# A row-wise gradient of an 8192 x 8192 matrix: partitions that hold 64 consecutive rows instead of six

## The chip, the core and the metric

The kernel runs on one core of a Trainium2 chip. Times are microseconds of device time. The kernel before takes 1245.38 us, the median of three runs (1245.34 to 1245.58). All other numbers come from one profiled execution of the same kernel.

The core has on-chip memory of 128 partitions. Its compute engines work on all partitions at once; here VectorE (DVE in the profile) and GpSimd (POOL) are used. Data come from and go to the chip's main memory by DMA: 16 DMA engines move the data of a transfer together, and SyncE (SP) issues the transfers one after the other on one queue.

## The reference

```python
def setup_inputs():
    return {"x": np.random.randn(8192, 8192).astype(np.float32)}

def reference(x):
    return np.gradient(x, axis=1)
```

Each row is treated by itself. In the inside of a row, out[j] = (x[j+1] - x[j-1]) / 2; at its two ends, out[0] = x[1] - x[0] and out[8191] = x[8191] - x[8190]. Input and output are 256 MB (268.44 million bytes) each, and a row is 32 KB.

## The kernel before

A tile holds two rows (R = 2) in each of 128 partitions: 256 rows, 64 KB a partition, 8.39 MB in all. There are nsets = 32 tiles. The function `sets` (lines 26 to 32) says which rows of the matrix a tile holds: three tiles (NB = 3) form a group, and a group takes 768 consecutive rows, of which each partition has six, rows 6p to 6p+5 of the group. The first tile of the group takes the first two of the six, the second the next two, the third the last two. So within a tile the partitions' pieces lie 6 x 32 KB = 192 KB apart in main memory, and each piece is one run of 64 KB. The last group has only two tiles, hence four rows a partition and 128 KB between pieces. Input and output use the same layout.

On the chip there are three buffers, slot0 to slot2, used in turn. For each tile:

- `load` (line 53) issues one transfer for the tile on SP (line 55). It waits until the store from the same buffer, three tiles earlier, has landed.
- GpSimd computes the four end values of each partition (two rows, two ends) into a small tile `ends` (line 65). It waits for the load.
- VectorE does the whole inside with one custom instruction (line 71): the difference of the buffer shifted by two elements, times 0.5. It writes the same buffer 64 elements further to the front, and waits for GpSimd.
- The four end values are put in their places over the result (line 82), by GpSimd for 12 of the tiles and by VectorE for the other 20.
- SP issues the store (line 84) as soon as they are there.

The order of the work is written out by hand. SP issues three loads, then three stores, each when its tile is done, then the next three loads, and so on: after every third tile the next three loads follow (lines 86 to 88). All 64 transfers go through SP's one queue in this order. The helper `chain` (line 43) only tells the tile framework which earlier steps an instruction must wait for.

Of the kernel before, what the change touches and what calls it, by code (L numbers as in the profile page):

```python
# [1 line left out]

# [4 lines left out]


@with_exitstack
def kernel(  # L10
    ctx: ExitStack,
    tc: tile.TileContext,
    x: bass.AP,
    out: bass.AP,
):
    nc = tc.nc
    P = nc.NUM_PARTITIONS
    n, m = x.shape
    R = 2
    NB = 3  # L20
    SH = 64
    W = R * m
    nsets = n // (P * R)
    f32 = x.dtype

    def sets(a):
        found = []
        for first in range(0, nsets, NB):
            q = min(NB, nsets - first)
            rows = a[first * P * R : (first + q) * P * R, :].rearrange("(p q) m -> p (q m)", p=P)  # L30
            found += [rows[:, k * W : (k + 1) * W] for k in range(q)]
        return found

    x_sets, out_sets = sets(x), sets(out)

    pool = ctx.enter_context(tc.tile_pool(name="pool", bufs=1))
    pad = pool.tile([P, 32], f32, name="pad", tag="pad")
    slots = [pool.tile([P, SH + W], f32, name=f"slot{k}", tag=f"slot{k}") for k in range(NB)]
    ends = pool.tile([P, nsets, R, 2], f32, name="ends", tag="ends")
    loads, stores = [], [None] * nsets  # L40
    in_front = {}

    def chain(i, ins, *needed):
        group, engine = f"slot{i % NB}", ins.ins.engine
        keep = [o.ins for o in needed]
        if in_front.get(engine, (None,))[0] == group:
            keep.append(in_front[engine][1])
        tc.declare_no_dep(ins.ins, group=group, keep=keep, reason="implied by the needed step")
        tc.add_to_no_dep_group(group, ins.ins)
        in_front[engine] = group, ins.ins  # L50
        return ins

    def load(i):
        b = slots[i % NB]
        ins = nc.sync.dma_start(out=b[:, SH : SH + W], in_=x_sets[i])  # L55
        loads.append(chain(i, ins, *([stores[i - NB]] if i >= NB else [])))

    with tc.manual_schedule():
        for i in range(NB):
            load(i)  # L60
        for i in range(nsets):
            b = slots[i % NB]
            xin = b[:, SH : SH + W].rearrange("p (t m) -> p t m", m=m)

            ins = nc.gpsimd.tensor_sub(  # L65
                out=ends[:, i, :, :],
                in0=xin[:, :, 1 : m : m - 2],
                in1=xin[:, :, 0 : m - 1 : m - 2],
            )
            at = [chain(i, ins, loads[i])]  # L70
            ins = nc.vector._custom_dve(  # L71
                dve_ops.TENSOR_TENSOR_REDUCE_SUB_MAX,
                out=b[:, 1 : W - 1],
                in0=b[:, SH + 2 : SH + W],
                in1=b[:, SH : SH + W - 2],
                s0=0.0,
                s1=0.5,
            )
            halved = chain(i, ins, *at)
            res = b[:, 0:W].rearrange("p (t m) -> p t m", m=m)  # L80
            placer = nc.gpsimd if i % 5 in (1, 3) and i < nsets - 2 else nc.vector
            ins = placer.tensor_copy(out=res[:, :, 0 : m : m - 1], in_=ends[:, i, :, :])  # L82
            placed = chain(i, ins, halved)
            ins = nc.sync.dma_start(out=out_sets[i], in_=b[:, 0:W])
            stores[i] = chain(i, ins, placed)
            if i % NB == NB - 1:
                for k in range(i + 1, min(i + 1 + NB, nsets)):
                    load(k)


# [1 line left out]
_INS = ['x']  # L92
_OUTS = [((8192, 8192), 'float32')]


# [23 lines left out]
```

## Time and profile before

| what | value |
|---|---|
| median of three runs | 1245.38 us |
| the profiled execution, its own time | 1246.23 us |
| its span in the profile | 1244.3 us |
| VectorE busy | 554.6 us, 45% of the span |
| GpSimd busy | 8.9 us, 1% |
| data moved | 268.44 MB read, 268.44 MB written |
| mean rate | 431 GB/s |
| issue to landing, median | load 57.9 us, store 40.4 us |

The span is what the profiler saw from the first to the last instruction; 1.93 us of the execution's own time lie around it. The profile's second part cuts the span in 40 slices and gives for each the busy share of an engine in tenths, so that 9 means 90% or more; for DMA it is the mean over the 16 engines. The third part adds up the packets, the pieces into which the transfers were cut. The DMA view can be asked for a window of time and then gives the same lines for the packets that start in it, also cut in 40 slices. Waits are listed as who waited for whom: total time, number of times, longest.

### The profile page before, as it was taken

The page shows a single profiled execution, that of the slowest core. Times are in us where ns is not written, and L with a number is a line of the kernel's source. Part 1 is how long each engine was busy: PE and PEld are TensorE (multiplying, and loading weights), DVE is VectorE, ACT ScalarE, POOL GpSimd, SP SyncE. Part 2 cuts the span into 40 slices and gives each one's busy share as a digit, 9 for nine tenths or more (in the row PEclk, how much of TensorE's full clock was granted, in tenths as well). Part 3 has the DMA queues.
Part 4 walks back from the last instruction along what each step waited for, and adds up shares of the span by engine and source line. Part 5 has one row for each costly group of instructions (what it writes and reads, how often), then busy time and mean ns, then how long its engine had stood idle before and what let it go on. Part 6 is the DMA issues. An engine that isn't in the chain of part 4 may idle for free.

```text
span 1244.3 us, 237 instructions
## 1 busy us (share of the span) xinstructions
DVE 554.6 (45%) x52; POOL 8.9 (1%) x48
## 2 busy tenths in 40 slices
DVE  2850583069009603850582079009603840591082
POOL 0000000000000000000000000000000000000000
DMA  9999999999999999999999999999999999999999
GB/s 404 438 436 423 421 438 438 438 438 436 434 423 430 434 438 438 430 436 432 428 434 436 432 436 434 438 436 430 432 428 438 436 434 438 434 434 430 430 409 404
DMA packets 9217, 536.88 MB, mean 431 GB/s; under 512 B 1024, under 2 KB 1024, under 8 KB 1024
## 3 DMA queue, kind: packets, MB, share of 16 engines
q1 hardware_dynamic: 9216, 536.88, 99.8%
q14 instruction: 1, 0.01, 0.0%
HBM read 268.44 MB, written 268.44 MB: 431 GB/s over the span
## 4 chain that ended last, share of the span: by engine, by line
another core or an unknown queue 74%; DVE 18%; DMA 3%; issue 2%; POOL 1%; SPq 0%; POOLq 0%
DVE slot L71 18%; DMA slot<-in_x_dram 3%; POOL ends L65 0%; POOL slot L82 0%; SPq L55 0%; POOLq L114 0%; DVE slot L82 0%
## 5 line engine op out<-in xcount | busy, mean ns | idle before, releaser
L71 DVE CUSTOM_DVE_ANT_0 slot<-slot 128x16382 f32<-128x16382 f32 x32 | 551.2, 17224 | 667.2 <-POOL ends L65 667.2
L65 POOL TENSOR_TENSOR ends<-slot 128x4 f32<-128x4 f32 x32 | 6.4, 200 | 988.1 <-DMA slot<-in_x_dram 988.1
L82 POOL COPY slot<-ends 128x4 f32<-128x4 f32 x12 | 2.3, 192 | 207.9 <-DVE slot L71 207.9
L82 DVE COPY slot<-ends 128x4 f32<-128x4 f32 x20 | 3.4, 172 | 0.7
L103 POOL MEMSET const-bfloat16-1.0<- 128x1 bf16 x1 | 0.1, 102 | 0.0
L103 POOL MEMSET const-uint8-127<- 128x1 uint8 x1 | 0.1, 102 | 0.0
L103 POOL MEMSET const-float32-0.0<- 128x1 f32 x1 | 0.1, 99 | 0.2 <-issue 0.2
L103 POOL MEMSET const-float32-1.0<- 128x1 f32 x1 | 0.1, 99 | 0.0
## 6 DMA issues: line engine op xcount, KB each, us to landing
slot<-in_x_dram SPq DMA_DIRECT2D x32, 57.9
out_dram<-slot SPq DMA_DIRECT2D x32, 40.4
```

The lines of the kernel that those rows point to most:

```text
L65: ins = nc.gpsimd.tensor_sub(out=ends[:, i, :, :], in0=xin[:, :, 1 : m : m - 2], in1=xin[:, :, 0 : m - 1 : m - 2],)
L71: ins = nc.vector._custom_dve(dve_ops.TENSOR_TENSOR_REDUCE_SUB_MAX, out=b[:, 1 : W - 1], in0=b[:, SH + 2 : SH + W], in1=b[:, SH : SH + W - 2],
L82: ins = placer.tensor_copy(out=res[:, :, 0 : m : m - 1], in_=ends[:, i, :, :])
L103: nc = _bacc.Bacc("TRN2", target_bir_lowering=False, num_devices=1)
```

## The change

The function `sets` loses its loop over groups. The whole matrix is laid out at once: partition p holds rows 64p to 64p+63, and tile k takes rows 2k and 2k+1 of those 64 in every partition. A tile's piece in a partition is still one run of 64 KB, but the pieces of neighbouring partitions are now 64 x 32 KB = 2 MB apart, in the input and in the output, for all 32 tiles. Nothing else is changed; the instructions on each engine and their order are the same, and the lines of the kernel after `sets` move up by four.

```diff
     def sets(a):
-        found = []
-        for first in range(0, nsets, NB):
-            q = min(NB, nsets - first)
-            rows = a[first * P * R : (first + q) * P * R, :].rearrange("(p q) m -> p (q m)", p=P)
-            found += [rows[:, k * W : (k + 1) * W] for k in range(q)]
-        return found
+        rows = a.rearrange("(p q) m -> p (q m)", p=P)
+        return [rows[:, k * W : (k + 1) * W] for k in range(nsets)]
 
     x_sets, out_sets = sets(x), sets(out)
```

## The prediction

> **What bounds the kernel now.** I read the page first, then the DMA view in short windows, then the waits.
>
> The page, parts 1 to 3 and 5:
>
> ```profile
> span 1244.3 us, 237 instructions
> DVE 554.6 (45%) x52; POOL 8.9 (1%) x48
> DMA  9999999999999999999999999999999999999999
> ...
> DMA packets 9217, 536.88 MB, mean 431 GB/s; under 512 B 1024, under 2 KB 1024, under 8 KB 1024
> q1 hardware_dynamic: 9216, 536.88, 99.8%
> ...
> L71 DVE CUSTOM_DVE_ANT_0 slot<-slot 128x16382 f32<-128x16382 f32 x32 | 551.2, 17224 | 667.2 <-POOL ends L65 667.2
> ```
>
> The 16 DMA engines are busy for 99.8% of the span in every slice; VectorE, the only compute engine with real work, is busy for 45%. Of the 9216 packets 1024 are tiny (under 512 B, 16 for each of 64 transfers). The other 8192 carry the 536.87 MB: 65,536 bytes each, one packet for one partition's two rows. Each of the 16 engines so moves 512 of them.
>
> The DMA view in four windows: the first wave of loads, the loads behind it, a stretch in the middle, and the last store.
>
> ```profile
> DMA packets 16, 1.05 MB, mean 350 GB/s; under 512 B 0, under 2 KB 0, under 8 KB 0
> q1 hardware_dynamic: 16, 1.05, 104.6%
> ...
> DMA packets 112, 7.34 MB, mean 465 GB/s; under 512 B 0, under 2 KB 0, under 8 KB 0
> q1 hardware_dynamic: 112, 7.34, 107.2%
> ...
> DMA  0999000999000999000999000999000999000999
> DMA packets 128, 7.34 MB, mean 459 GB/s; under 512 B 16, under 2 KB 16, under 8 KB 16
> ...
> DMA packets 160, 8.39 MB, mean 387 GB/s; under 512 B 32, under 2 KB 32, under 8 KB 32
> q1 hardware_dynamic: 160, 8.39, 89.2%
> ```
>
> Packets are counted where they start, so share x window x 16 engines / packets is the mean duration of one.
> - 1.2 to 4.2 us (first wave, one packet per engine): 1.046 x 3.0 x 16 / 16 = 3.138 us.
> - 4.2 to 20 us: 1.072 x 15.8 x 16 / 112 = 2.420 us.
> - 300 to 316 us: the digits repeat every six slices of 0.4 us, three busy and three empty. All 16 engines start their packets within about half a packet's time of each other, every 2.4 us: they walk in step.
> - 1222.6 to 1244.3 us (the last store, 128 large packets): 0.892 x 21.7 x 16 / 128 = 2.420 us.
>
> 512 x 2.420 = 1239.0 us of the 1244.3 us span. So the bound is each engine's own 2.42 us for 64 KB, and the memory behind it never shows except in two waves: the first loads, and the first stores, at 57.9 to 59.2 us:
>
> ```profile
> DMA packets 16, 1.05 MB, mean 807 GB/s; under 512 B 0, under 2 KB 0, under 8 KB 0
> q1 hardware_dynamic: 16, 1.05, 264.4%
> ```
>
> 2.644 x 1.3 x 16 / 16 = 3.437 us per packet.
>
> The waits of SP's queue show what hangs on landings:
>
> ```profile
> SPq L84 <- DVE slot L82: 525.5, 20, 55.9
> SPq L55 <- DMA out_dram<-slot: 372.9, 29, 19.1
> ```
>
> SP waits often, but always with transfers already queued behind which it waits, since the DMA row has no gap.
>
> **The change part by part.**
>
> *What stays.* The 32 loads, 32 stores and all compute instructions stand in the same order on every engine; each transfer is still 128 runs of 64 KB, so still 512 large packets per engine. No wait, buffer or instruction is added or taken: 0 us. That VectorE needs 17.22 us per tile is hidden under the 2 x 8 x 2.42 = 38.7 us that its load and store take; longer packets only widen this cover. SP's waits on landings stretch in proportion to the packets, with the queue no emptier.
>
> *The last two tiles* had runs 128 KB apart and now have them 2 MB apart; the other 30 go from 192 KB to 2 MB. These are one edit: the addresses that the 16 engines touch at the same moment.
>
> *Price of the new addresses.* The 128 partitions of a transfer now begin at multiples of 2 MB: whatever share of them an engine has, 16 engines in step read addresses equal in their low 21 bits. Before, with 192 KB = 3 x 64 KB, those bits differed from engine to engine. If memory spreads addresses over its parts by such bits, the engines now meet in the same few parts. No row of before shows a 2 MB step, so I bound it.
> - From below: the last store, with a power of two (128 KB) between runs, has 2.420 us per packet, as the tiles with 192 KB. By this row the change costs 0, and no gain is possible beyond the 1244.3 - 1239.0 = 5.3 us that are not plain packet time; of those at least the 1.2 us before the first transfer starts remain, so 4.1 us at most.
> - From above: the only packets that memory rather than the engine lengthened are the two waves: 3.138 - 2.420 = 0.718 us more for loads, 3.437 - 2.420 = 1.017 us more for stores. At the store wave's price throughout it is 512 x 1.017 = 520.7 us.
>
> I take the loads' price for all packets. The waves are the rows where 16 engines press on memory that cannot serve them at once, the condition that the change would make permanent; the 128 KB row has a step 16 times smaller. A part of each wave is a cost of beginning or of turning round that steady traffic would not repeat, so I take the lower of the two, also for stores. The first wave has already paid: 511 x 0.718 = 366.9 us.
>
> *Weighed against the Trainium skill.* The Trainium skill, "DMA: Bandwidth & Descriptors", section "Latency and other measured facts", gives for copies of 128-partition tiles 207 GB/s per direction at a row pitch of 512 KiB, 164 at 2 MiB, 103 at 4 MiB and 214 where the pitch is padded; it calls channel aliasing its inference. By the ratio 214/164 the time would be an estimated 1245.4 x 1.305 = 1625 us. Its runs were 16 KiB, not 64 KB, and no run of before has such a pitch; the 128 KB row neither bears it out nor speaks against it.
>
> *Sum.* The profiled execution took 1246.23 us, 1.93 us of it outside its span of 1244.3 us. 1246.2 + 366.9 = 1613.1 us; the median of the runs shown, 1245.38 us, lies 0.85 us lower, so I forecast 1612 us. The last large packet still ends the program: its wave is in the 512.
>
> **The rivals.**
>
> *Only a part of the traffic pays.* (a) Stores may be taken up by buffers and loads alone pay: 255 x 0.718 = 183 us, 1428 us. (b) The step may break: an engine that is held back falls behind the others, reaches a given address later, and meets nobody. For it: at 600 to 616 us the pulses of before have widened over the whole period (next fence), by drift alone. If only the first three loads and three stores pay (48 packets per engine): 47 x 0.718 = 34 us, 1279 us; of these the loads alone: 23 x 0.718 = 17 us, 1262 us. Against it: at 300 us the engines were still in step within about 1.2 us of 2.42, after 120 packets each, and a crowd of engines that waits for one place moves on together.
>
> ```profile
> DMA  9997709997709997709993909993739993739993
> ```
>
> *The pitch does not matter* (not slower). The memory has headroom that the engines' 431 GB/s do not use up, or mixes high address bits so that 2 MB steps spread as 192 KB steps do. For it: the 128 KB row, and 2.42 us all through the loads behind the first wave, though the engines are in step. Then each packet stays 2.42 us and the time stays 1245.4 us. It decides as soon as memory serves 16 such streams at 16 x 65,536 B / 2.42 us = 433 GB/s; below that every shortfall lands on the end, for nothing covers DMA time. A gain could only come from shorter waves: two waves of before cost 0.7 and 1.0 us, and without all of it and the other gaps 1246.2 - 4.1 - 0.85 = 1241.3 us is the floor.
>
> *Dearer than the waves.* If more than 16 requests pile up at one place, a packet may exceed 3.437 us: over 1245.4 + 520.7 = 1766 us. Nothing in the trace holds such a packet on average, so this has little weight.
>
> *The change does not do what it says.* Then the 64 KB runs would be cut up; but a tile's two rows are adjacent in the new layout too, so I give this nothing.
>
> **How the numbers follow.** This kernel's runs agree within 0.02%; about 0.2% (2.5 us) is what a measurement can tell from no change. All traffic pays about a wave's price (1430 to 1766 us; likeliest, 1612): 0.56. A part pays (1262 to 1430): 0.24. A trace of it, 1248 to 1262: 0.02. The pitch does not matter: 0.09. Faster, down to 1241: 0.03. Dearer than 1766: 0.06. The range 1262 to 1766 holds 0.80 and ends on the two bounds worked out above. Slower is 0.56 + 0.24 + 0.02 + 0.06 = 0.88, same 0.09, faster 0.03.
>
> **What would show it.** Right: packets still 9216 and 536.88 MB, DMA digits still 9 throughout, but GB/s per slice near 536.88 MB / 1610 us = 333 instead of 434, packets of about 3.1 us by the same working, VectorE's busy time unchanged at 554.6 us with its share down to about 34%, and SP's wait on landed stores up by some 30%. Case (a) would show loads at 3.1 us and stores at 2.42 in the windows; case (b) a low GB/s in the first slices that climbs back to 434. Wrong: packets at 2.42 us in every window; or stretches in which the DMA row falls below 9, which would mean that a wait and not the packets holds the end.

## The result: 4.7% slower, a sixth of the loss that was forecast

The changed kernel takes 1304.97 us (median of six runs, 1294.97 to 1311.88) against 1245.74 us for the kernel before (six runs, 1245.34 to 1246.48). The ratio is 1.0466, with a 95% interval from 1.0425 to 1.0508. The forecast was 1612 us. The direction was right and the time lies in the range, but the loss is 59 us and not 367. The runs of the changed kernel also scatter over 17 us, those of the kernel before over 1 us.

The page of the changed kernel, parts 1 to 3 and the costliest group:

```profile
span 1298.8 us, 237 instructions
DVE 554.6 (43%) x52; POOL 8.8 (1%) x48
DMA  9999999999999999999999999999999999999988
GB/s 355 412 416 383 400 434 434 386 432 430 434 400 430 422 426 406 428 432 404 432 428 436 402 428 434 414 418 436 424 418 436 422 432 410 434 434 416 420 299 303
DMA packets 9217, 536.88 MB, mean 413 GB/s; under 512 B 1024, under 2 KB 1024, under 8 KB 1024
q1 hardware_dynamic: 9216, 536.88, 99.2%
...
L67 DVE CUSTOM_DVE_ANT_0 slot<-slot 128x16382 f32<-128x16382 f32 x32 | 551.2, 17224 | 711.1 <-POOL ends L61 711.1
```

Packets, bytes and VectorE's time are what they were, and the DMA engines are still busy 99.2% of a longer span (1298.8 us, 54.5 us more). So the packets became longer, as forecast; but only some of them. The row of GB/s shows which: it is low in the first slices (355), climbs to the old 434, dips in every third or fourth slice (383, 386, 400, 406, 404 are the first), and ends with 299 and 303.

The DMA view of the changed kernel in four windows: the first wave (1.2 to 4.2 us), the packets behind it (4.2 to 20), a stretch in the middle (190 to 206) and one in the last two stores (1252 to 1268). Packets are counted where they start.

```profile
DMA packets 16, 1.05 MB, mean 350 GB/s; under 512 B 0, under 2 KB 0, under 8 KB 0
q1 hardware_dynamic: 16, 1.05, 115.9%
...
DMA packets 92, 6.03 MB, mean 382 GB/s; under 512 B 0, under 2 KB 0, under 8 KB 0
q1 hardware_dynamic: 92, 6.03, 101.6%
...
DMA  9709399909399909399909399909379909379939
DMA packets 116, 6.95 MB, mean 434 GB/s; under 512 B 10, under 2 KB 10, under 8 KB 10
q1 hardware_dynamic: 116, 6.95, 100.2%
...
DMA  0049940000999000009994000999900009999400
DMA packets 80, 5.24 MB, mean 328 GB/s; under 512 B 0, under 2 KB 0, under 8 KB 0
q1 hardware_dynamic: 80, 5.24, 97.7%
```

Share x window x 16 / large packets gives 3.477 us in the first wave (3.138 before), 1.016 x 15.8 x 16 / 92 = 2.792 us behind it, 1.002 x 16 x 16 / 106 = 2.420 us in the middle, and 0.977 x 16 x 16 / 80 = 3.126 us in the last stores. The two DMA rows show the difference between the last two. In the middle the 16 engines start at all times of the 2.4 us period: only single slices are empty. In the last stores there are three to five slices of 0.4 us in which nobody starts: the engines are in step. The same 2 MB step costs nothing in the one state and 0.7 us a packet in the other.

The time of each packet beyond 2.418 us, added up from the single packet records of the trace, gives 49.5 us per engine (2.9 us before). Of these 13.9 us fall in the first 140 us: 6.7 us in the first three loads, 5.3 us where the first three stores give way to loads, the rest in these stores. Another 9.9 us fall in the last two stores, and 25.7 us in between, all of it where the direction changes: 21.4 us at the nine places where stores give way to loads, 4.3 us where loads give way to stores. So about 31 of the 49.5 us lie at changes of direction. There the packets are longer than in step; around the first such change, from 122 to 132 us:

```profile
DMA packets 52, 2.62 MB, mean 262 GB/s; under 512 B 12, under 2 KB 12, under 8 KB 12
q1 hardware_dynamic: 52, 2.62, 101.7%
```

1.017 x 10 x 16 / 40 = 4.07 us, and the longest single packet there takes 5.2 us. The loss falls from change to change, from 5.3 us at the first and 3.5 at the second to 1.5 us at the last from stores to loads, while the landings of one transfer on the 16 engines spread from 4 to 16 us.

Ahead of the last two stores the engines are idle for 7.3 us on average (1.7 us before), as the store of the last tile but one waits for VectorE while the engines, now apart, run out of loads. 46.6 + 5.6 = 52.2 us of the 54.5 us are found so. Of the rest, the records show 0.7 us more of idle time at the end and 0.6 us more in the first 10 us; about 1 us stays unplaced.

SP's waits grew as the packets did:

```profile
SPq L80 <- DVE slot L78: 537.7, 20, 58.3
SPq L51 <- DMA out_dram<-slot: 395.8, 29, 23.2
```

The second was 372.9 us: 6% more, not the 30% that the forecast named.

### The profile page after: what moved, and what is told of

It reads as the page before. It is cut to its first block, busy times and chain, and to the rows that moved or that the text cites. A ratio compares the mean times of both kernels' runs of the same rounds, so it can differ in the third digit from the quotient of the medians.

```text
span 1298.8 us, 237 instructions
## 1 busy us (share of the span) xinstructions
DVE 554.6 (43%) x52; POOL 8.8 (1%) x48
## 2 busy tenths in 40 slices
DMA packets 9217, 536.88 MB, mean 413 GB/s; under 512 B 1024, under 2 KB 1024, under 8 KB 1024
## 3 DMA queue, kind: packets, MB, share of 16 engines
q1 hardware_dynamic: 9216, 536.88, 99.2%
## 4 chain that ended last, share of the span: by engine, by line
another core or an unknown queue 74%; DVE 17%; DMA 4%; issue 2%; POOL 1%; SPq 0%; POOLq 0%
DVE slot L67 17%; DMA slot<-in_x_dram 4%; POOL ends L61 0%; POOL slot L78 0%; SPq L51 0%; POOLq L110 0%; DVE slot L78 0%
```

## The experiments

Three theories are tested. Theory A: the step of 2 MB lengthens a packet only while the 16 engines start together; they drift apart by themselves, and meet again after every dry queue, that is, whenever all transfers that were issued are done. Theory B: what costs is the reach of a transfer over the whole 256 MB, whatever the step. Theory C: at a change of direction, reads and writes in flight together collide at alike addresses.

**Is it the power of two, or the reach?** Three kernels differ from the kernel before only in the number of tiles in a group of `sets` (with 16 and 8 in the place of 31 for the other two).

```diff
-        for first in range(0, nsets, NB):
-            q = min(NB, nsets - first)
+        for first in range(0, nsets, 31):
+            q = min(31, nsets - first)
```

> The 32 tiles in a group of 31 and a group of one: the pieces of a tile lie 31 x 64 KB = 1984 KB apart (64 KB in the last tile), not 2048 KB; nothing else differs from the changed kernel. Theory A (alike addresses: engines in step meet in the same part of memory because the step is a power of two) expects packets of 2.42 us and 1246 us, within 0.2% of the kernel before. Theory B (the far reach: a transfer that touches the whole 256 MB costs more, power of two or not) expects about the changed kernel's 1305 us.

Measured: 1245.95 us, ratio to the kernel before 0.9999 (0.9990 to 1.0008). The DMA view of this kernel from 4.2 to 20 us:

```profile
DMA  0990000993000993000797000797000399000099
DMA packets 112, 7.34 MB, mean 465 GB/s; under 512 B 0, under 2 KB 0, under 8 KB 0
q1 hardware_dynamic: 112, 7.34, 107.2%
```

The engines are in step (two or three slices with starts, three or four without) and each packet takes 2.420 us. A step shorter by 3% takes away the whole loss, with nearly the same reach. Theory B is out.

> Groups of 16 tiles: 1024 KB between pieces, half the step of the changed kernel. Theory A with a memory that tells addresses apart by bits around 20 to 23 expects less than at 2 MB: between 1246 and 1290 us, and the last two stores between 2.42 and 3.04 us a packet. Theory B (far reach) expects half of the loss, some 1275 us, falling in proportion to the step.

Measured: 1285.24 us, ratio 1.0334 (1.0287 to 1.0381). From 1250 to 1266 us, in the last stores, 80 packets at a share of 97.4% give 0.974 x 16 x 16 / 80 = 3.117 us, as with 2 MB. Theory A had the total right, but had expected at most 3.04 us for these packets.

> Groups of eight tiles: 512 KB between pieces. Theory A expects 1246 to 1255 us, next to nothing, if the bits that tell parts of memory apart lie above; theory B expects a quarter of the loss, 1260 us.

Measured: 1259.56 us, ratio 1.0109 (1.0092 to 1.0126), more than theory A gave it. This time happens to be that of theory B, and the one at 1024 KB lies 10 us above what B gave it; the 1984 KB run decides against B all the same. The DMA view at 512 KB, in the last stores (1230 to 1246 us):

```profile
DMA  3000093000093000093000093000093000093000
DMA packets 113, 6.36 MB, mean 397 GB/s; under 512 B 16, under 2 KB 16, under 8 KB 16
q1 hardware_dynamic: 113, 6.36, 91.7%
```

All 16 engines start within two slices, in step, and 0.917 x 16 x 16 / 97 = 2.420 us: at 512 KB being in step costs nothing. Its packet records lose 14.8 us per engine, nearly all where the direction changes: 8.6 us from stores to loads and 5.3 us from loads to stores. So the loss has two parts, and they begin at different steps.

**Does the loss go when the engines begin apart?** Ahead of the first load, seven small ones are to keep pairs of engines busy for different times:

```diff
-        for i in range(NB):
-            load(i)
+        early = []
+        for k in range(2, 16, 2):
+            ins = nc.sync.dma_start(out=slots[2][8 * k : 9 * k, SH : SH + 10240], in_=x_sets[2][8 * k : 9 * k, 0:10240])
+            early.append(chain(2, ins))
+        load(0)
+        load(1)
+        load(2, *early)
```

(`load` takes further steps to wait for.)

> The changed kernel (2 MB), with seven small loads ahead of the first: 40 KB in each of 2, 4, ... 14 partitions of tile 2, so that pairs of engines begin the first large load at eight different times. Tile 2 is loaded again in full afterwards. Theory A expects packets of 2.42 to 2.55 us from the first load on (the changed kernel had 2.85 us on average in its first load, 2.67 and 2.57 in the next two) and so most of the 12 us that the first six transfers lost per engine back, less some 6 to 9 us for the extra bytes and issues. A rival, that the first load is slow because memory is cold, expects the large packets of the first load at 2.85 us as before.

Measured: 1316.65 us in a single run, slower than the changed kernel; the expectation on the first load was missed. While the small loads ran, the large packets were slow, 6.2 to 8.0 us for those that start before 25 us: a cost of this edit whose cause stays open. So the run decides nothing about the first load; that cold memory does not make it slow is shown at 1984 KB, whose packets behind the first wave take 2.420 us. Once they were through, the packets show what the run was for. From 34 to 50 us:

```profile
DMA  9399397799393999393999377999373999773979
DMA packets 121, 7.01 MB, mean 438 GB/s; under 512 B 14, under 2 KB 14, under 8 KB 14
q1 hardware_dynamic: 121, 7.01, 101.1%
```

1.011 x 16 x 16 / 107 = 2.419 us, with starts in every slice. Between 34 and 120 us this kernel loses 0.1 us per engine, the changed one 3.5 us. Apart, the engines pay nothing here; but the run mixes this with a cost of its own, so it supports theory A and does not prove it.

**Which direction pays?** The layouts of input and output are set apart (neither kernel gives the rows their right places, so they serve for timing alone):

```diff
-    x_sets, out_sets = sets(x), sets(out)
+    x_sets, out_sets = sets(x, nsets), sets(out, NB)
```

(`sets` takes the number of tiles in a group as its second argument; the other run has NB for the input and nsets for the output.)

> Loads as in the changed kernel (2 MB between pieces), stores as in the kernel before (192 KB): the rows of the result go to other places of the output, everything else is computed and moved as before. Theory A (engines in step, each direction by itself) expects the loads' own share: some 6 to 10 us in the first three loads, 2.42 us a packet in the last two stores, and a small loss where stores give way to loads: 1255 to 1265 us. Theory C (the loss where stores give way to loads comes from reads and writes that are in flight together at alike addresses, and needs both steps) expects no loss at all at those places: packets of 2.42 us at 120, 240, 360 us. A rival, that loads at 2 MB are slow whenever the direction changes, expects there the 3 us per change that the changed kernel shows.

Measured: 1266.70 us, ratio 1.0169 (1.0152 to 1.0186). The first three loads lose 7.4 us in the records, the last two stores run at 2.42 us, the first change from store to load loses 1.7 us and the nine others 0.3 to 0.9 us each. The changes from load to store lose as much here, 0.2 to 0.9 us each. So this run's total is a little above theory A's, and theory C, which expected no loss at the changes, is missed.

> The other half: loads 192 KB apart, stores 2 MB apart (the rows of the result go to other places of the output). Theory A expects 2.42 us in the first three loads and 3.04 us in the last two stores, 10 us per engine; with theory C no loss where the direction changes, so 1256 to 1262 us. The rival that a change of direction costs by the stores' step alone expects some 3 us at each of ten changes on top, 1285 to 1295 us.

Measured: 1326.14 us, ratio 1.0638 (1.0591 to 1.0684). With stores alone at 2 MB the kernel is 21 us slower than with both. All expectations were too low, and the reason is the clearest sight of being in step. This kernel's stores at 85 to 101, 345 to 361 and 590 to 606 us, and behind them the first stores of the changed kernel at 86 to 102 us:

```profile
DMA  9990000499900009994000099950000999400099
DMA packets 102, 5.64 MB, mean 352 GB/s; under 512 B 16, under 2 KB 16, under 8 KB 16
q1 hardware_dynamic: 102, 5.64, 104.9%
...
DMA  4999300999900499900089990009998008999400
DMA packets 112, 6.29 MB, mean 393 GB/s; under 512 B 16, under 2 KB 16, under 8 KB 16
q1 hardware_dynamic: 112, 6.29, 98.9%
...
DMA  9799339799339799339799339799739997939399
DMA packets 121, 7.08 MB, mean 442 GB/s; under 512 B 13, under 2 KB 13, under 8 KB 13
q1 hardware_dynamic: 121, 7.08, 103.3%
...
DMA  7797979397797797499797097798898849779979
DMA packets 116, 6.75 MB, mean 422 GB/s; under 512 B 13, under 2 KB 13, under 8 KB 13
q1 hardware_dynamic: 116, 6.75, 101.2%
```

The runs of empty slices go from four to two or three to none, and the packet from 1.049 x 16 x 16 / 86 = 3.12 us to 2.64 to 2.45 us. Loads at 192 KB leave the engines in step, so the first three stores pay in full: 13.7 us per engine up to their last two packets. The changed kernel writes to the same places at that time, but its loads have shaken the engines apart: its packets take 1.012 x 16 x 16 / 103 = 2.52 us, and it loses some 2 us. Stores alone did not part the engines here: in 21 packets in a row the mean stays between 2.9 and 3.2 us. The changes from stores to loads cost 6.9 us at first and 1.5 to 2.4 us at the last four. Theory C falls in the form given: a change of direction costs here too, with only one side at 2 MB.

**Does a new start bring the loss back?** Two runs. The first was to make each group of loads wait for the third store of the group before:

```diff
-                    load(k)
+                    load(k, stores[i])
```

> The changed kernel in which each group of three loads also waits until the third store before it has landed: the queue runs dry once a group and all 16 engines begin again together. Theory A expects each group to lose what the first lost, some 7 us in its three loads and more in its stores, so 9 x 7 to 9 x 12 us on top of the waits: 1360 to 1440 us, with the loads' packets at 2.7 to 2.85 us after each restart. If being in step is not the cause, only the waits are added, about 2 to 3 us for each of ten groups: 1325 to 1335 us, and the loss at the changes of direction may even go, as nothing is mixed there.

Measured: 1306.07 us, the time of the changed kernel. It tells nothing: the wait did not come about. SP issued the fourth load at 87.98 us, 2.65 us after it had issued the third store, while that store landed only between 126 and 131 us. So the run is in effect a repeat of the changed kernel, and whether a new start in mid-program brings the loss back stays untested.

The second shows it from the other side: it keeps the queue from running dry before the last stores.

```diff
-            if i % NB == NB - 1:
-                for k in range(i + 1, min(i + 1 + NB, nsets)):
+            if i % NB == 1 and i + 2 < nsets:
+                for k in range(max(i + 1, NB), i + 1 + NB):
                     load(k)
```

> The changed kernel with the groups of loads moved, so that the order is three loads, two stores, two loads, and from then on three stores and three loads, and the program ends on three stores with two loads still queued when the first of them is issued. The queue does not run dry before the last stores, so the engines do not begin them together. Theory A expects the last two stores at 2.42 to 2.5 us a packet instead of 3.04, and with the idle time before them gone 12 to 15 us less than the changed kernel: about 1290 us. The rival that the last stores are slow for where they lie in memory, or because nothing else is in flight, expects them at 3.04 us again and 1300 to 1305 us.

Measured: 1299.13 us, ratio 1.0412 (1.0387 to 1.0437). The DMA view of this kernel in the last stores (1262 to 1278 us):

```profile
DMA  3377993373993373993373993373993373993373
DMA packets 115, 6.62 MB, mean 414 GB/s; under 512 B 14, under 2 KB 14, under 8 KB 14
q1 hardware_dynamic: 115, 6.62, 95.4%
```

No slice is empty, and 0.954 x 16 x 16 / 101 = 2.418 us. The last stores are slow in the changed kernel because the engines begin them together; the rival (their place, or nothing else in flight) is out. But the kernel's median is 6 us lower and not 12 to 15, and as the two intervals overlap, even these 6 us are not clear of the scatter. Engines that have drifted apart also end apart: in the records they finish between 1279.9 and 1296.2 us, on average 7.6 us before the last. The window from 1280 to 1298 us of this kernel (length, VectorE, GpSimd, clock, DMA share, GB/s):

```profile
1280.00:1298.00 18.00, 0.00 (x0) 0.00 (x0) 1.00 0.43 186
```

So the idle time ahead of the last stores has moved to the end. And the packets of the whole kernel lose 49.5 us per engine, as in the changed kernel: the 9.9 us saved in the last stores are lost again at the changes from stores to loads, 36.0 us against 26.7. In the repeat of the changed kernel these changes lost 34.5 us, so this may be no more than the difference from run to run.

**What does a change of direction cost?** After the second store, one load follows each store, so that the direction changes at each transfer:

```diff
-            if i % NB == NB - 1:
-                for k in range(i + 1, min(i + 1 + NB, nsets)):
-                    load(k)
+            if i >= 1 and i + 2 < nsets:
+                load(i + 2)
```

> The changed kernel with loads and stores in turns: from the third store on, one load follows each store, so that the direction changes with each transfer and not with each third. Theory C expects the loss at a change from store to load, about 2.7 us per engine, at 29 places and not at ten: some 51 us more than the changed kernel, 1340 to 1370 us. Theory A alone expects no more loss than in the changed kernel, 1270 to 1310 us.

Measured: 1363.26 us, ratio 1.0942 (1.0898 to 1.0987), 58 us more than the changed kernel; the records lose 112.0 us per engine.

> The kernel before (192 KB) with loads and stores in turns, as the run with 2 MB: if what that run lost, 58 us more than the changed kernel, is due to the step of 2 MB, this one stays within 5 us of the kernel before, 1245 to 1250 us. If the order itself makes it slow (a queue that runs dry at each turn), it loses about the same, some 1300 us.

Measured: 1246.94 us, ratio 1.0005 (0.9995 to 1.0015). The order itself is free. So with 2 MB each of the 19 added changes from store to load, together with the change back, costs about 58 / 19 = 3 us on average, and with 192 KB nothing.

**A version that beats both?** The order that ends on three stores, with the layout of the kernel before:

> The kernel before (192 KB) with the same order. Its queue ran dry for 1.7 us per engine ahead of the last two stores and nothing else is lost there, so 1.5 to 2 us less than the kernel before: about 1244 us, 0.1 to 0.2% faster or no change that can be told.

Measured: 1245.87 us, ratio 0.9997 (0.9988 to 1.0006): no difference that can be told. The last two stores run at 2.418 us without a gap ahead of them, but here too the engines end apart, 1.8 us before the last on average (0.3 us in the kernel before), which takes the gain.

## Why the prediction was right and wrong

*The bound: right, the cover nearly.* Packets, bytes and VectorE's time stayed, and 46.6 of the 54.5 us sit in the DMA engines' packets with nothing to hide them. But the forecast had the queue "no emptier", with VectorE wholly hidden. Before, the engines were already idle for 1.7 us ahead of the last two stores, and now for 7.3 us.

*The price of a packet in step: right in size, in part by luck.* The forecast took 3.138 us from the first wave of before. Measured where the engines are in step at 2 MB: 3.126 us in the last stores, 3.12 us in the stores of the kernel with only these at 2 MB. That the wave of before is slow for the same reason is not shown: the changed kernel's own first wave takes 3.477 us, more than either. Being in step with a step of 192, 512 or 1984 KB costs nothing behind the first wave.

*How many packets pay: wrong, and this is the step that failed.* The forecast said that the change would make the waves' condition "permanent" and multiplied by 511. The measured excess, 46.6 us per engine, is that of 46.6 / 0.718 = 65 packets. In place of a lasting crowd, the runs show engines that part within the first loads. The middle of the program then runs at 2.42 us with all pieces 2 MB apart, and only the packets in step and those at the changes of direction pay. In the records the landings of one transfer on the 16 engines lie 1.6 us apart in the first load and over 10 us by the middle of the program. The argument that a crowd which waits for one place moves on together held for stores (21 packets in a row at about 3.1 us) and not for loads. The sign was there to be read: the digits of before at 600 us had already spread over the whole period without any such delay.

*Rival (b), that the step may break: the right mechanism, priced too low.* It had 34 us for one group of loads and stores at most. In that group the records lose 13.9 us, the change to the next loads included. It left out two terms: 25.7 us at the other changes of direction, where even parted engines lose 3.5 to 1.5 us each time that stores give way to loads; and the last two stores, which begin together after a dry queue, with 9.9 us in packets and 5.6 us more of idle time ahead of them. The time lies in the band that the forecast gave to a part of the traffic paying (1262 to 1430), but not by its terms. The sign that it named, a rate low at first that climbs back to 434, is in the page.

*Rival (a), loads alone pay: wrong.* Stores pay as much for a packet in step, and for longer.

*The pitch does not matter, and faster: wrong*, as the run at 1984 KB shows by its contrast. *Dearer than the waves: wrong* for the time, but single packets at the first change of direction did take up to 5.2 us, more than the 3.437 us of the store wave of before.

*The rule of the Trainium skill* ("DMA: Bandwidth & Descriptors", section "Latency and other measured facts") fits the stretches in step and not the program. It gives 164 GB/s per direction at 2 MiB; twice that is an estimated 328 GB/s, and the last stores show 328 GB/s. These stores go one way only, with pieces of 64 KB, so the equal numbers may be chance. Over the whole program the rate is 413 GB/s. Its inference, aliasing of streams in lock step, fits the runs as far as the lock step goes, which is the condition to look for: at 1024 KB the packets in step are as slow as at 2 MB (3.117 us), at 512 KB they are not. What happens inside memory no run here shows.

*Left open:* why parted engines lose time where the direction changes, which is the larger part of the loss (about 31 of 49.5 us), why this falls in the course of the program, and why it begins at a smaller step (it is there at 512 KB, where being in step is free). The runs show where it is, what it costs and that it goes at 192 and 1984 KB, not what it is.

## What to carry to other kernels

A row's price and the number of instructions that pay it are two readings: before a stall is multiplied by all packets, ask whether the state that causes it keeps itself up. In these kernels a step of 1024 or 2048 KB between the partitions' pieces cost time in two states: where the DMA engines began together (at the start, and after the dry queue ahead of the last stores), and where the direction changed, there at 512 KB too. A step beside the power of two (1984 KB for 2048) removed all of it. And a queue that does not run dry keeps engines parted, but parted engines also end apart.

## What was not expected of the hardware

- Loads at alike addresses part the engines within some 20 packets (3.48 us in the first wave, 2.55 us from 48 to 58 us, in the third load); stores keep them in step for at least 21 packets at about 3.1 us.
- Two slowed directions cost less than one: 1305 us with loads and stores at 2 MB, 1326 us with stores alone. In the first three stores the records show why: the loads' own delay has parted the engines and spares them (some 2 us lost against 13.7).
- A change from store to load costs 5.3 us at first and 1.5 us at the last in the changed kernel, and nothing at 192 KB, though engines are apart there too (the landings of one transfer lie 0.5 to 3 us apart).
- The changed kernel's times scatter by 1.3%, those of the kernel before by 0.1%: how the engines part differs from run to run. The trace of the repeat lost 34.5 us at the changes from stores to loads, that of the changed kernel 26.7 us; that this makes the scatter is inferred.
